# A decoder layer's mixing in five pieces of columns for six, with its feed-forward groups kept

## The chip, the cores and the metric

The kernel runs on one core of a Trainium2 chip. The metric is the device time of one execution in microseconds (us). A core has five engines, each with an instruction queue of its own that is worked off in order: the TensorE (PE, matmuls; PEld is its loading of weights), the VectorE (DVE), the ScalarE (ACT), the GpSimd (POOL) and the SyncE (SP), which here starts the DMA transfers. A median measured against the kernel before is told from no change from about 0.2% on.

## The reference

One layer of a hybrid decoder: RMSNorm, one input projection for four retention heads and four HGRN2 heads, their chunkwise recurrence, a gated output projection added to the input, RMSNorm, a squared-ReLU feed-forward of width 4096 added on, and a final RMSNorm. There are 2048 prompt tokens and 64 sample tokens (8 sequences of 8 with states of their own), 2112 in all; the model width is 1024. The outputs are the normed activations of both and the recurrences' final states.

```python
def mixer(h, pos, s_ret, s_hg, w_in, ret_norm_w, hgrn_norm_w, lb, w_out):
    proj = h @ w_in                                   # 1024 -> 4096 columns
    rq, rk, rv, rg, hq, hf, hi, hg = jnp.split(proj, idx, axis=-1)
    ...
    o_r, s_ret_new = chunk_gla(rq, rk, rv, log_g_ret, s_ret)
    ...
    o_h, s_hg_new = chunk_gla(hq, k_in, v_in, log_f, s_hg)
    ...
    o = jnp.concatenate([o_r, o_h], axis=-1).astype(h.dtype)
    return o @ w_out, s_ret_new, s_hg_new

def reference(...):
    ...
        hp = rmsnorm(xp, norm_mix_w[l])
        mp, sr_p, sh_p = mixer(hp, pos_p, zero_ret, zero_hg, ...)
        xp = xp + mp
        hp = rmsnorm(xp, norm_ffn_w[l])
        xp = xp + jnp.square(jax.nn.relu(hp @ w_up[l])) @ w_down[l]
    ...
    y_prompt = rmsnorm(xp, final_norm_w)
```

## The kernel before

**Precision.** All products are of 32-bit floats. Each operand is cut into a high part (a cast on the ScalarE) and a low part (the rest, a subtraction on the VectorE), and a product is three matmuls: high by high, high by low, low by high. Weights are cut as they arrive, 128 x 1024 at a time: hi at L271 on the ScalarE, lo at L285 on the VectorE, from a buffer `raw` that a transfer of 512 KB fills.

**Groups.** The tokens are columns. They are worked on in three groups of T = 640, 768 and 64 + 640 = 704 (the last with the sample tokens), first all groups through the mixing, then all through the feed-forward. [...] `proj()` (L342) makes one block of 128 output rows: for each of the operands, for each of the three part products, a matmul for each piece, into one of two banks `pj`.

**Mixing.** A group goes through `norm_in`, the heads' projections and recurrences, and `out_proj`. `norm_in` of the next group runs beside `out_proj` of this one: for each of eight blocks the ScalarE makes a high part (L546), the VectorE a low part (L547), the ScalarE a square and the VectorE its sum (L530). `residual()` makes the first seven heads' share of eight output blocks, 21 part products each, and adds the input (L1204); `out_proj` then adds the eighth head's share (L1249), stores the sum as `res` and scaled by the norm's weights as `in` in DRAM, one store for each of eight blocks. For the first group the squares are summed apart, on POOL and VectorE (L530, L600), and a matmul with ones makes their column sums (L570).

**Feed-forward.** It is a Strassen-like scheme of seven products for eight. Activations are quartered by rows and by halves of columns, B11 to B22; `plan_operands` sums them (L1291) and cuts the sums (L1280 on the ScalarE, L1284 on the VectorE) into the operands T3, T2, T1, T4 of the products, two row blocks each. `product()` (L1189) is 24 matmuls of T/2 columns. `up_two` starts a group with the fourteen products of the first two blocks of the width: B11, B11, B21, B22, B21, B22, then T2, T3, T1, T4 twice; a product's two banks are in `pj` or `pf`. T4's product adds onto T3's bank after T3 was read, by the second add at L1406 (u3, followed on the VectorE by the sum at L1436).

**The end of a group.** `finish()` makes the final norm of a feed-forward group, while the next group's feed-forward runs: eight squares (ACT, L1625), six adds and two adds of a guard term (DVE, L1627 and L1630), two splits (ACT L1356, DVE L1357), column sums by eight matmuls (L1365), two factors (ACT, L1676), sixteen products (DVE, L1643), and eight stores of y on SP.

**What sets the order.** Nothing is put in order by hand. Work beside the matmuls is put on an agenda by `later(ticks, ...)`, and a tick passes with every operand of `proj` (three part products) and with every two matmuls of the feed-forward. So for `finish()`, `begin`, `pace`, `wait` and `each` are ticks after the next group's start: a square every `pace` from `begin`, a product every `each` from `wait`, and a tick of the feed-forward is two matmuls. Engines run their queues in the order in which the program issues, so an instruction that waits holds up all behind it.

**Memory.** A tile of T columns takes one of 44 slabs of 768 columns; there are six load buffers of the same width. Weights in the feed-forward are loaded to a pool `raw` of 3 buffers or, two positions in seven of three each, a pool `sum` of 4 (by the weight's number, k % 7 % 2).

## Time and profile before

| | |
|---|---|
| median of 3 runs | 2508.93 us (2508.18 to 2508.98) |
| the profiled execution | 2508.95 us |
| its span, first to last instruction | 2507.2 us |
| granted TensorE clock | 0.999 |
| busy: PE, DVE, ACT, POOL | 2494.0, 1878.1, 1253.9, 366.1 us |
| DMA moved | 525.39 MB, mean 210 GB/s |

A row of the timeline gives the start of an instruction in us from the span's start, its duration in us, its engine and line, the operation, the tiles that it writes and reads with their sizes, how many alike follow each other, and in brackets how long the engine sat idle before it and who ended that. Tile names are the program's with their buffer's number left out: `slab` any of the slabs, `pj` and `pf` the banks of matmul results, `ld` a load buffer, `hi`, `lo` and `raw` a weight's parts and source. A row of the chain gives a start, a time and the number of instructions in it. Windows give a stretch's length and each engine's busy time in it, with the number of instructions in brackets. Line numbers are those of the kernel before; the changed file's are a little higher (L342 is L345, L285 is L288, L1204 is L1214, L1406 is L1421, L1643 is L1658).

### The profile page before, as it was taken

How to read it: one execution, taken by the hardware profiler on the slowest of the kernel's cores; microseconds unless marked ns; L12 is line 12 of the kernel's file. 1: busy time of each engine (PE TensorE's matmuls, PEld its weight loads, DVE VectorE, ACT ScalarE, POOL GpSimd, SP SyncE). 2: the span in 40 equal slices, each digit the busy share in tenths (PEclk: the TensorE clock that was granted, in tenths of full speed). 3: DMA queues.
4: the chain of work that ended last, by engine and by line, in shares of the span. 5: the costliest groups of instructions: out<-in, count | busy, mean ns of one | idle time of the engine just before them, and what ended most of it. 6: DMA issues, size and time to landing. Idle time of an engine off the chain costs nothing.

```text
span 2507.2 us, 41510 instructions
## 1 busy us (share of the span) xinstructions
PE 2494.0 (99%) x16593; PEld 2474.9 (99%) x16593; DVE 1878.1 (75%) x2443; ACT 1253.9 (50%) x1674; POOL 366.1 (15%) x304
## 2 busy tenths in 40 slices
PE   9999999999999999999999999999999999999998
PEld 9999999999999999999999999999999999999998
DVE  7666865668684766677775899775699878678987
ACT  6665653444463444443644555444454436445544
POOL 5223304324411432340000000000000000000000
PEclk9999999999999999999999999999999999999999
DMA  7454563465575565758866856566675546867552
GB/s 269 164 185 168 209 225 135 160 228 185 199 244 212 194 215 195 264 206 306 305 216 213 284 198 213 173 237 221 202 261 177 189 148 202 274 192 247 192 187 88
DMA packets 189073, 525.39 MB, mean 210 GB/s; under 512 B 18640, under 2 KB 59856, under 8 KB 188880
## 3 DMA queue, kind: packets, MB, share of 16 engines
q1 hardware_dynamic: 188736, 522.73, 60.6%
q8 instruction: 130, 2.13, 0.3%
q14 instruction: 63, 0.52, 0.1%
q10 hardware_dynamic: 144, 0.02, 0.0%
HBM read 389.50 MB, written 132.38 MB: 208 GB/s over the span
## 4 chain that ended last, share of the span: by engine, by line
PE 96%; DVE 3%; ACT 1%; issue 1%; DMA 0%; DVEq 0%; ACTq 0%
PE pj L342 27%; PE pf L1189 26%; PE pj L1189 25%; PE pjv L732 8%; PE mm L898 1%; PE po L1078 1%; PE mm L1086 1%; PE po L1080 1%; PE mm L955 1%; PE mm L509 1%; PE mm L510 1%; PE mm L1012 1%; PE mm L830 0%; PE po L764 0%; DVE raw L1221 0%
## 5 line engine op out<-in xcount | busy, mean ns | idle before, releaser
L271 ACT CAST hi<-raw 128x1024 fp32r<-128x1024 f32 x392 | 413.1, 1054 | 610.0 <-PE pf L1189 261.4
L342 PE MATMUL pj<-slab,hi 128*128 128x320 f32 (+2 forms) x3072 | 661.5, 328 | 2.6 <-DVE slab L644 1.3
L1189 PE MATMUL pf<-slab,hi 128*128 128x320 f32 (+2 forms) x2768 | 659.1, 321 | 0.0
L1189 PE MATMUL pj<-slab,hi 128*128 128x352 f32 (+2 forms) x2608 | 622.1, 322 | 0.0
L285 DVE TENSOR_TENSOR lo<-raw,hi 128x1024 fp32r<-128x1024 f32 x392 | 485.3, 1238 | 111.9 <-ACT hi L271 105.8
L342 PEld LDWEIGHTS pj<-slab,hi 128*128 128x128 f32 x3072 | 508.1, 188 | 5.3 <-DVE slab L644 1.5
L1189 PEld LDWEIGHTS pf<-slab,hi 128*128 128x128 f32 x2768 | 481.9, 188 | 0.0
L1189 PEld LDWEIGHTS pj<-slab,hi 128*128 128x128 f32 x2608 | 454.5, 188 | 0.1
L1189 PE MATMUL pf<-slab,lo 128*128 128x320 f32 (+2 forms) x1384 | 445.5, 322 | 0.0
L1189 PE MATMUL pj<-slab,lo 128*128 128x352 f32 (+2 forms) x1304 | 420.3, 322 | 0.0
L342 PE MATMUL pj<-slab,lo 128*128 128x320 f32 (+2 forms) x1536 | 379.1, 328 | 0.4 <-DVE lo L285 0.4
L342 PEld LDWEIGHTS pj<-slab,lo 128*128 128x128 f32 x1536 | 263.3, 188 | 1.3 <-DVE lo L285 0.9
L1189 PEld LDWEIGHTS pf<-slab,lo 128*128 128x128 f32 x1384 | 260.3, 188 | 0.0
L1189 PEld LDWEIGHTS pj<-slab,lo 128*128 128x128 f32 x1304 | 245.3, 188 | 0.0
L732 PE MATMUL pjv<-hi,slab 128*128 128x256 f32 x1088 | 204.8, 285 | 0.0
L1280 ACT CAST slab<-slab 128x640 fp32r<-128x640 f32 (+2 forms) x192 | 145.7, 780 | 65.8 <-DVE slab L1291 52.2
L1284 DVE TENSOR_TENSOR slab<-slab 128x640 fp32r<-128x640 f32 (+2 forms) x192 | 167.3, 886 | 8.9 <-PE pj L1189 3.2
L732 PEld LDWEIGHTS pjv<-hi,slab 128*128 128x128 f32 x1088 | 172.2, 192 | 1.5 <-issue 0.2
L732 PE MATMUL pjv<-lo,slab 128*128 128x256 f32 x544 | 153.8, 283 | 0.0
L879 ACT ACTIVATE slab<-slab 128x640 f32<-128x640 f32 (+2 forms) x72 | 56.4, 784 | 154.6 <-POOL slab L875 154.4
L732 PEld LDWEIGHTS pjv<-lo,slab 128*128 128x128 f32 x544 | 104.2, 192 | 0.0
L1536 DVE TENSOR_TENSOR slab<-pf,slab 128x640 f32<-128x640 f32 (+2 forms) x88 | 77.6, 888 | 29.6 <-PE pf L1189 29.1
(218 smaller groups left out, 3004.1 us busy)
## 6 DMA issues: line engine op xcount, KB each, us to landing
raw<-w SPq DMA_DIRECT2D x264, 512.0 KB, 4.2
slab<-u SPq DMA_DIRECT2D x32, 384.0 KB, 4.7
u<-ld SPq DMA_DIRECT2D x30, 384.0 KB, 3.7
slab<-u SPq DMA_DIRECT2D x32, 352.0 KB, 4.5
u<-ld SPq DMA_DIRECT2D x30, 352.0 KB, 4.0
slab<-u SPq DMA_DIRECT2D x32, 320.0 KB, 4.5
u<-ld SPq DMA_DIRECT2D x30, 320.0 KB, 3.9
ld<-x SPq DMA_DIRECT2D x16, 384.0 KB, 3.6
```

The source lines that it names most:

```text
L271: self.nc.scalar.copy(hi, raw)
L285: self.nc.vector.tensor_tensor(out=lo, in0=self.second.pop(j), in1=hi.bitcast(F32), op=ALU.subtract)
L342: self.nc.tensor.matmul(pj[:, i, :T2], w, a[:, c0:c1], start=j == 0 and q == 0, stop=j == n - 1 and q == 2)
L509: self.nc.tensor.matmul(ps, self.ones_r, hi, start=True, stop=False)
L510: self.nc.tensor.matmul(ps, self.ones_r, lo, start=False, stop=True)
L732: nc.tensor.matmul(pj[:, i * 256:(i + 1) * 256], a[:, s:s + C], ww, start=kb == 0 and q == 0, stop=kb == KB - 1 and q == 2)
L879: nc.scalar.activation(x["dd", w][:, a:T], x["dd", w][:, a:T], AF.Exp)
L898: nc.tensor.matmul(ps[:, j * P:(j + 1) * P], qk[:, cols[c]], qk[:, cols[c]], start=True, stop=True)
L1189: self.nc.tensor.matmul(*a, **k)
L1280: self.nc.scalar.copy(hi[:, :g.T], B[name][:, :g.T])
L1284: self.nc.vector.tensor_tensor(out=lo[:, :g.T], in0=B[name][:, :g.T], in1=hi.bitcast(F32)[:, :g.T], op=ALU.subtract)
L1536: nc.vector.tensor_tensor(out=r, in0=ps, in1=r, op=ALU.add)
```

## The change

The mixing's groups become T = 512, 768 and 64 + 768 = 832. The first is one piece of 512 columns, the others two of 384 and of 416. The feed-forward keeps 640, 768 and 704, now as `FF_GROUPS`. What the mixing hands on in DRAM (`res` and `in`) is therefore kept in tiles between the edges 0, 512, 640, 1280, 1408 and 2112 of either grouping: the second and the third group store each block in two parts (32 more stores in all), and a load of a quarter that crosses an edge comes in two parts. Slabs grow to 832 columns and are 41 for 44, load buffers grow alike, `raw` has 2 buffers for 3 and shares by k % 3. `finish()` of the first two feed-forward groups starts at ticks 10 and 60 for 96 and 200, with closer steps. y is stored with its columns in one order for all groups.

```diff
@@ -26,8 +26,8 @@
 FF = 4096
 EPS = 1e-6
 C = 128
-SLAB = 768
-NSLAB = 44
+SLAB = 832
+NSLAB = 41
 NLD = 6
 LEVELS = (64, 32, 16, 8, 4, 2)
 NLV = len(LEVELS) + 2
@@ -35,8 +35,11 @@
-GROUPS = ((0, 0, 640), (0, 640, 768), (NS, 1408, 640))
+GROUPS = ((0, 0, 512), (0, 512, 768), (NS, 1280, 768))
 NT = NS + SEQ
+FF_GROUPS = ((0, 640), (640, 768), (1408, 704))
+
+EDGES = (0, 512, 640, 1280, 1408, NT)
 WT = 1024
 N_IN, N_OUT, N_UP, N_DN = 32, 8, 32, 32
 W_OUT0 = N_IN
@@ -259,9 +262,9 @@
                 if self.stream[self.w_load][0] == "p":
                     break
                 k, later = self.w_load, self.w_load >= self.n_sums
-                other = later and k % 7 % 2
+                other = later and k % 3
                 raw = self.raws[k] = self.wp.tile([P, WT], F32, tag="sum" if other else "raw", name="raw",
-                                                  bufs=4 if other else 3)
+                                                  bufs=4 if other else 2)
                 e = self.stream[k]
                 self.fetch(raw, self.sums[e[1]] if e[0] == "s" else self.I["w"][e[1]])
                 self.w_load += 1
@@ -426,6 +429,13 @@
                 g.pieces = [(0, g.T)] if g.T <= 512 else [(0, g.T // 2), (g.T // 2, g.T)]
                 g.segs = [list(range(first)), list(range(first, nch))]
                 gs.append(g)
+            fs = []
+            for off, T in FF_GROUPS:
+                g = type("G", (), {})()
+                g.i, g.off, g.T = len(fs), off, T
+                fs.append(g)
+            self.between = {(name, a): self.dp.tile([P, KB, e - a], F32, name=f"{name}{a}")
+                            for a, e in zip(EDGES, EDGES[1:]) for name in ("res", "in")}
             nc.scalar.dma_start(vec, I["vec"])
             nc.scalar.preload_act_table_set("natural_log_exp_and_others")
             self.norm_in(gs[0], True)
@@ -460,12 +470,12 @@
                 mixing.close()
                 self.pf = ctx.enter_context(tc.tile_pool(name="pf", bufs=2, space=bass.MemoryType.PSUM))
-            self.out_proj(gs[2], 3, lambda: self.prepare(gs[0], 12), end_of_mixing)
-            self.ffn(gs[0], lambda: self.prepare(gs[1], 8))
-            self.finish(gs[0], begin=96, pace=10, wait=200, each=8)
-            self.ffn(gs[1], lambda: self.prepare(gs[2], 8), 190)
-            self.finish(gs[1], begin=96, pace=10, wait=200, each=8)
-            self.ffn(gs[2], None, 190)
+            self.out_proj(gs[2], 3, lambda: self.prepare(fs[0], 12), end_of_mixing)
+            self.ffn(fs[0], lambda: self.prepare(fs[1], 8))
+            self.finish(fs[0], begin=10, pace=4, wait=60, each=5)
+            self.ffn(fs[1], lambda: self.prepare(fs[2], 8), 190)
+            self.finish(fs[1], begin=10, pace=4, wait=60, each=5)
+            self.ffn(fs[2], None, 190)
             nc.sync.dma_start(self.O["ret_p"].rearrange("h d v -> d h v"), self.S[:, :H])
             nc.sync.dma_start(self.O["hg_p"].rearrange("h d v -> d h v"), self.S[:, H:])
@@ -1242,22 +1252,27 @@
         nc, T = self.nc, g.T
         part = self.residual(g, when, beside)
         between()
-        g.res, g.in_ = (self.dp.tile([P, KB, T], F32, name=f"{name}{g.i}") for name in ("res", "in"))
         for n in N_ORDER:
             pj = self.proj(g, self.take(2), g.oc[H - 1])
             r, b = part[n], self.get()
             nc.vector.tensor_tensor(out=self.v2(r, g), in0=pj, in1=self.v2(r, g), op=ALU.add)
             nc.scalar.activation(b[:, :T], r[:, :T], AF.Copy, scale=self.vec[:, V_FFN + n:V_FFN + n + 1])
-            for kept, t in ((g.res, r), (g.in_, b)):
-                nc.sync.dma_start(kept[:, n], t[:, :T])
+            for name, t in (("res", r), ("in", b)):
+                for a, e in zip(EDGES, EDGES[1:]):
+                    if g.off <= a < g.off + T:
+                        nc.sync.dma_start(self.between[name, a][:, n], t[:, a - g.off:e - g.off])
         self.flush()
-    def quarter(self, g, src, v, m, h, into):
+    def quarter(self, g, name, v, m, h, into):
         n, w = 4 * m + 2 * v, g.T // 2
-        self.nc.sync.dma_start(self.pair(g, into), src[:, n:n + 2, h * w:(h + 1) * w])
+        c = g.off + h * w
+        for a, e in zip(EDGES, EDGES[1:]):
+            t0, t1 = max(a, c), min(e, c + w)
+            if t0 < t1:
+                self.nc.sync.dma_start(self.pair(g, into)[:, :, t0 - c:t1 - c], self.between[name, a][:, n:n + 2, t0 - a:t1 - a])
     def prepare(self, g, pace):
@@ -1265,7 +1280,7 @@
         def load(v, name):
             g.B[v][name] = self.load()
-            self.quarter(g, g.in_, v, *PLACE[name], g.B[v][name])
+            self.quarter(g, "in", v, *PLACE[name], g.B[v][name])
         for j, (name, v) in enumerate((name, v) for name in ("B11", "B21", "B22") for v in range(2)):
             first, second = self.halve(g, g.B[v], name, g.ops[v])
@@ -1295,7 +1310,7 @@
         def load(v, name):
             g.B[v][name] = self.load()
-            self.quarter(g, g.in_, v, *PLACE[name], g.B[v][name])
+            self.quarter(g, "in", v, *PLACE[name], g.B[v][name])
         for j, (name, v) in enumerate([(name, v) for v in range(2) for name in ("T3", "T2", "T1")] + [("T4", 0), ("T4", 1)]):
             self.later(10 + 8 * j, self.block_sum, g, g.B[v], name)
@@ -1315,7 +1330,7 @@
         def load(v, m, h):
             g.R[v][m, h] = self.get()
-            self.quarter(g, g.res, v, m, h, g.R[v][m, h])
+            self.quarter(g, "res", v, m, h, g.R[v][m, h])
         def square(v, m, h):
             t = self.get()
@@ -1663,8 +1678,9 @@
     def outputs(self, g, h):
-        o = KB * g.off
-        return self.O["y"][:, o:o + KB * g.T].rearrange("p (n h t) -> p n h t", n=KB, h=2)[:, :, h]
+        T2 = g.T // 2
+        a = g.off + h * T2
+        return self.O["y"].rearrange("p (n t) -> p n t", n=KB)[:, :, a:a + T2]
     def last_guard(self, g, q):
@@ -1796,7 +1812,7 @@
     samples, prompts, off = [], [], 0
     for ns, p0, n in GROUPS:
         T = ns + n
-        rows = y[:, KB * off:KB * (off + T)].reshape(P, KB, T).transpose(2, 1, 0).reshape(T, D)
+        rows = y.reshape(P, KB, NT)[:, :, off:off + T].transpose(2, 1, 0).reshape(T, D)
         samples.append(rows[:ns])
         prompts.append(rows[ns:])
         off += T
```

Two places in the order of the VectorE and one of the TensorE show what moves. First the TensorE at the program's beginning: the last of the first projection blocks' matmuls and the column sums of the squares (`mm`). Before:

```order
L342 MATMUL pj<-slab,hi 128x320 x4
L342 MATMUL pj<-slab,lo 128x320 x2
L342 MATMUL pj<-slab,hi 128x320 x4
L342 MATMUL pj<-slab,lo 128x320 x2
L570 MATMUL mm<-slab,ones 128x320 x2
L342 MATMUL pj<-slab,hi 128x320 x4
```

and now:

```order
L345 MATMUL pj<-slab,hi 128x512 x2
L345 MATMUL pj<-slab,lo 128x512
L345 MATMUL pj<-slab,hi 128x512 x2
L345 MATMUL pj<-slab,lo 128x512
L580 MATMUL mm<-slab,ones 128x512
L345 MATMUL pj<-slab,hi 128x512 x2
```

Two rows are an operand by a weight block, as before, with three matmuls for six; the column sums stand behind 66 matmuls for 132.

Second the VectorE at the start of the second feed-forward, from a sum for T4 to the second add at L1406 (L1421 in the change) and what follows. Before:

```order
L1291 TENSOR_TENSOR slab<-ld,slab 128x768
L285 TENSOR_TENSOR lo<-raw,hi 128x1024
L1284 TENSOR_TENSOR slab<-slab 128x768
L1406 TENSOR_TENSOR slab<-pj,slab 128x768
L285 TENSOR_TENSOR lo<-raw,hi 128x1024
L1630 TENSOR_TENSOR slab<-slab 128x320
L1436 TENSOR_TENSOR slab<-slab 128x768
L1406 TENSOR_TENSOR slab<-pj,slab 128x768
L285 TENSOR_TENSOR lo<-raw,hi 128x1024
L1627 TENSOR_TENSOR slab<-slab 128x640 x2
L1406 TENSOR_TENSOR ld<-pf,slab 128x768
L1406 TENSOR_TENSOR slab<-pf,slab 128x768
```

and now:

```order
L1658 SCALAR_TENSOR_TENSOR slab<-slab,vec 128x320 x3
L1299 TENSOR_TENSOR slab<-slab 128x768
L1306 TENSOR_TENSOR slab<-ld,slab 128x768
L1658 SCALAR_TENSOR_TENSOR slab<-slab,vec 128x320 x2
L288 TENSOR_TENSOR lo<-raw,hi 128x1024
L1299 TENSOR_TENSOR slab<-slab 128x768
L1658 SCALAR_TENSOR_TENSOR slab<-slab,vec 128x320 x2
L1421 TENSOR_TENSOR slab<-pf,slab 128x768
L1658 SCALAR_TENSOR_TENSOR slab<-slab,vec 128x320 x2
L288 TENSOR_TENSOR lo<-raw,hi 128x1024
L1658 SCALAR_TENSOR_TENSOR slab<-slab,vec 128x320 x4
L1421 TENSOR_TENSOR slab<-pf,slab 128x768
```

The sixteen products of the first group's final norm (L1643, now L1658) stand ahead of T3's eviction, twelve of them ahead of T2's; before they came after all of these. Its six adds and two splits (L1642, L1372) are further up, among the sums and cuts:

```order
L288 TENSOR_TENSOR lo<-raw,hi 128x1024
L1642 TENSOR_TENSOR slab<-slab 128x640
L1299 TENSOR_TENSOR slab<-slab 128x768
L1642 TENSOR_TENSOR slab<-slab 128x640
L1306 TENSOR_TENSOR slab<-ld 128x768
L288 TENSOR_TENSOR lo<-raw,hi 128x1024
L1642 TENSOR_TENSOR slab<-slab 128x640
L1372 TENSOR_TENSOR slab<-slab 128x640
L1299 TENSOR_TENSOR slab<-slab 128x768
L1306 TENSOR_TENSOR slab<-slab,ld 128x768
L288 TENSOR_TENSOR lo<-raw,hi 128x1024
L1372 TENSOR_TENSOR slab<-slab 128x640
```

Third the VectorE in the residual products of the first group, from the fourth eviction (L1204, now L1214) to the fifth and on. L547 and L530 are `norm_in` of the next group, L285 weights' cuts, L1174 and L350 the last head's gating and cuts. Before:

```order
L1204 TENSOR_TENSOR slab<-pj,ld 128x640
L530 TENSOR_TENSOR slab<-slab 128x768
L285 TENSOR_TENSOR lo<-raw,hi 128x1024
L547 SCALAR_TENSOR_TENSOR slab<-ld,vec,slab 128x768
L530 TENSOR_TENSOR slab<-slab 128x768
L1174 TENSOR_TENSOR slab<-slab 128x384
L547 SCALAR_TENSOR_TENSOR slab<-ld,vec,slab 128x768
L1174 TENSOR_TENSOR slab<-slab 128x384
L530 TENSOR_TENSOR slab<-slab 128x768
L1204 TENSOR_TENSOR slab<-pj,ld 128x640
```

and now:

```order
L1214 TENSOR_TENSOR slab<-pj,ld 128x512
L1184 TENSOR_TENSOR slab<-slab 128x256
L557 SCALAR_TENSOR_TENSOR slab<-ld,vec,slab 128x768
L1184 TENSOR_TENSOR slab<-slab 128x256
L540 TENSOR_TENSOR slab<-slab 128x768
L557 SCALAR_TENSOR_TENSOR slab<-ld,vec,slab 128x768
L1214 TENSOR_TENSOR slab<-pj,ld 128x512
L540 TENSOR_TENSOR slab<-slab 128x768
L353 TENSOR_TENSOR slab<-slab 128x512
L288 TENSOR_TENSOR lo<-raw,hi 128x1024
L353 TENSOR_TENSOR slab<-slab 128x512
L557 SCALAR_TENSOR_TENSOR slab<-ld,vec,slab 128x768
```

`norm_in`'s instructions (L557, L540) keep their 768 columns and the weights' cuts (L288) their 1024; the group's own are 512 and 256 wide for 640 and 384.

## The prediction

> **What bounds the kernel now.** First the page, its busy shares and the chain that ended last:
>
> ```profile
> PE 2494.0 (99%) x16593; PEld 2474.9 (99%) x16593; DVE 1878.1 (75%) x2443; ACT 1253.9 (50%) x1674; POOL 366.1 (15%) x304
> PE 96%; DVE 3%; ACT 1%; issue 1%; DMA 0%; DVEq 0%; ACTq 0%
> PE pj L342 27%; PE pf L1189 26%; PE pj L1189 25%; PE pjv L732 8%; PE mm L898 1%; PE po L1078 1%; PE mm L1086 1%; PE po L1080 1%; PE mm L955 1%; PE mm L509 1%; PE mm L510 1%; PE mm L1012 1%; PE mm L830 0%; PE po L764 0%; DVE raw L1221 0%
> ```
>
> The TensorE is the bound, nearly without a gap. Its waits (total us, times, longest) are the next view:
>
> ```profile
> PE pj L342 <- DVE slab L644: 1.3, 1, 1.3
> PE pj L342 <- ACT hi L271: 0.7, 1, 0.7
> PE pj L342 <- DVE slab L1204: 0.5, 1, 0.5
> ```
>
> So a matmul that is left out is worth its whole interval, and nothing else can be won: there is hardly any waiting to remove. The VectorE at 75% looks harmless, but that is an average; the windows (length, then busy time of PE, PEld, DVE, ACT, POOL, the granted clock, DMA share, GB/s) over the five stretches that the change touches say more:
>
> ```profile
> 7.93:27.24 19.31, 19.30 (x128) 18.89 (x129) 16.54 (x15) 14.77 (x20) 6.06 (x3) 1.00 0.81 304
> 302.60:341.70 39.10, 39.10 (x283) 39.09 (x282) 35.70 (x63) 27.70 (x43) 1.50 (x1) 1.00 0.66 216
> 713.10:760.10 47.00, 46.48 (x294) 46.19 (x293) 40.08 (x60) 26.12 (x40) 0.00 (x0) 1.00 0.76 258
> 1593.04:1630.50 37.46, 37.46 (x218) 37.46 (x217) 28.94 (x31) 23.36 (x28) 0.00 (x0) 1.00 0.54 174
> 2062.70:2097.30 34.60, 34.60 (x217) 34.60 (x216) 24.78 (x28) 20.96 (x27) 0.00 (x0) 1.00 0.54 178
> ```
>
> They are the start, the residual products of groups 0 and 1, and the starts of the second and third feed-forward. In the second row the VectorE works 35.70 of 39.10 us.
>
> **The matmuls saved.** The projection's matmuls (L342) take, by the chain of waits, in runs of 320, 384, 352 columns, and the values' (L732) of 256:
>
> ```profile
> 75.14 5.87 PE pj L342 x40
> 437.39 6.96 PE pj L342 x40
> 893.81 4.75 PE pj L342 x30
> 111.55 14.03 PE pjv L732 x117
> ```
>
> That is 146.8, 174.0, 158.3 and 119.9 ns each: columns at 2.4 per ns (133.3, 160.0, 146.7, 106.7) and a rest of 13.2 to 14.0 that doesn't grow with the columns. I take 13.3, and so 226.7 ns for 512 columns and 186.7 for 416, an estimate by that line. Each group has 768 products of a weight block with an operand half at L342, in two pieces 1536 matmuls, 4608 in the three groups; group 0's 512 columns go in one piece, so 768 + 2 x 1536 = 3840 are left, over the same columns in all. Gain: 768 x 13.3 ns = **10.2 us**. Hardly anything in the rows speaks for less than 9 or more than 11.
>
> [...]
>
> **Start of the second feed-forward.** The change calls finish() with begin=10, wait=60 where it was 96 and 200, and so puts group 0's final norm (six adds L1627, two splits L1357, sixteen products L1643) in among the sums L1291 and lower halves L1284 that the VectorE makes for the products T2, T3, T1, T4. T4, the tenth product, adds onto T3's bank, so its first matmul waits for T3's eviction, the second add at L1406. Rows of the timeline (start, duration, idle before):
>
> ```profile
> 1598.34 1.23 DVE L285 TENSOR_TENSOR lo<-raw,hi 128x1024 fp32r<-128x1024 f32 x1 [2.93 <-ACT hi L271]
> 1599.77 0.96 DVE L1284 TENSOR_TENSOR slab<-slab 128x768 fp32r<-128x768 f32 x1 [0.21 <-ACT slab L1280]
> ...
> 1602.50 1.23 DVE L285 TENSOR_TENSOR lo<-raw,hi 128x1024 fp32r<-128x1024 f32 x1 [0.90 <-ACT hi L271]
> ...
> 1606.37 0.96 DVE L1284 TENSOR_TENSOR slab<-slab 128x768 fp32r<-128x768 f32 x1 [0.91 <-ACT slab L1280]
> ...
> 1614.98 1.23 DVE L285 TENSOR_TENSOR lo<-raw,hi 128x1024 fp32r<-128x1024 f32 x1 [0.79 <-ACT hi L271]
> ...
> 1618.85 0.96 DVE L1284 TENSOR_TENSOR slab<-slab 128x768 fp32r<-128x768 f32 x1 [0.91 <-ACT slab L1280]
> ...
> 1626.55 0.96 DVE L1406 TENSOR_TENSOR slab<-pj,slab 128x768 f32<-128x768 f32 x1 [0.59 <-PE pj L1189]
> ```
>
> ```profile
> 1650.71 0.82 DVE L1357 TENSOR_TENSOR slab<-slab 128x640 fp32r<-128x640 f32 x1
> 1651.44 0.95 DVE L1381 SCALAR_TENSOR_TENSOR slab<-slab 128x768 f32<-128x768 f32 x1
> 1652.31 0.95 DVE L1406 TENSOR_TENSOR ld<-pj,slab 128x768 f32<-128x768 f32 x1
> 1667.26 2.40 DVE L1643 SCALAR_TENSOR_TENSOR slab<-slab,vec 128x320 f32<-128x320 f32 x5
> 1669.57 0.95 DVE L1464 TENSOR_TENSOR slab<-pf,slab 128x768 f32<-128x768 f32 x1
> ```
>
> ```profile
> 1630.51 0.51 PE L1189 MATMUL pj<-slab,hi 128*128 128x384 f32 x2
> ```
>
> Back to back, instructions start closer than their durations: 0.73 us for a 640-wide one (1650.71 to 1651.44), 0.87 for 768 (1651.44 to 1652.31), 0.46 for L1643 (five in 2.31). The adds at L1627 are 640 wide like L1357. Now 6 x 0.73 + 2 x 0.73 + 16 x 0.46 = 13.2 us come ahead of T3's eviction, and the sum at L1436 (0.87) goes behind it: 12.3 more. The idle stretches quoted after the first, 4.3 us, can take part of it; the first (2.93) can't, as by the order all of this work stands behind the lower half that ends it. The eviction, done before at 1627.5, is done at 1627.5 + 12.3 - 4.3 = 1635.5. T4 began at 1630.51, and the eight matmuls of the norm's column sums now ahead of it take 8 x 0.147 = 1.2: 1631.7. Loss 3.8, taken as **4 us**; 2.5 if L1643's stores and the ScalarE's squares leave no new holes, 6 if half of the old holes stay, since the stores are queued on SP ahead of weight loads.
>
> **Start of the third.** The same with a 768-wide norm and 704-wide operands, and with less cover:
>
> ```profile
> 2070.50 1.22 DVE L285 TENSOR_TENSOR lo<-raw,hi 128x1024 fp32r<-128x1024 f32 x1 [0.85 <-ACT hi L271]
> ...
> 2093.70 1.22 DVE L285 TENSOR_TENSOR lo<-raw,hi 128x1024 fp32r<-128x1024 f32 x1 [1.04 <-ACT hi L271]
> ...
> 2096.91 0.88 DVE L1406 TENSOR_TENSOR slab<-pj,slab 128x704 f32<-128x704 f32 x1
> ```
>
> ```profile
> 2138.71 1.67 DVE L1643 SCALAR_TENSOR_TENSOR slab<-slab,vec 128x384 f32<-128x384 f32 x3
> 2140.33 0.89 DVE L1464 TENSOR_TENSOR ld<-pf,slab 128x704 f32<-128x704 f32 x1
> ```
>
> ```profile
> 2097.89 0.55 PE L1189 MATMUL pj<-slab,hi 128*128 128x352 f32 x2
> ```
>
> The eviction ended at 2096.91 + 0.88 = 2097.8 and T4 began 0.1 later: no slack is left today. There come in 6 x 0.87 + 2 x 0.87 + 16 x 0.54 (three in 1.62) = 15.6 us; between the two rows of L285 seven idle stretches of 0.85 to 1.04 lie, 7 us in all. Eviction at 2106.4, T4 ready at 2097.9 + 8 x 0.174 = 2099.3: 7.1, and with a few tenths of new holes **7.5 us**; bounds 5 and 9.
>
> **Residual products of group 0.** norm_in of group 1 runs on the VectorE beside them, 768 wide as before, but a product block now passes in 21 x 0.2267 = 4.8 us instead of 42 x 0.1468 = 6.2. In the window of 39.10 us lie six blocks, 37.0, and 2.1 of other matmuls; now 28.6 + 2 = 30.6. The VectorE's 35.70 there shrinks less: by the order, two small copies and two state updates fewer (0.7), nine evictions and halves of 640 to 512 columns (0.13 each by the step from 768 to 640: 1.2), six of 384 to 256 and two left behind the stretch (1.7): 32.1. It is now the longer one, with 3.4 us in which it sat idle in that window, mostly for the ScalarE. Two banks cover one block's lateness, and before they were needed already:
>
> ```profile
> 302.59 0.82 DVE L1204 TENSOR_TENSOR slab<-pj,ld 128x640 f32<-128x640 f32 x1
> 333.20 0.82 DVE L1204 TENSOR_TENSOR slab<-pj,ld 128x640 f32<-128x640 f32 x1
> ```
>
> Four blocks (24.7 us of matmuls and up to 2.1 others) apart, but 30.6 us: 4 of the 6.2 were used. With 4.8 of cover and 32.1 + 3.4 against 30.6 I take **5 us**; 0 if holes and cover swallow it, 8 if the VectorE carries lateness in from the mixing ahead.
>
> **Smaller terms.** Residual products of group 1: norm_in of group 2 grows from 704 to 832 columns, fifteen instructions by 0.13 = 2 us in a window where 40.08 of 47.00 are busy and where L342 waited for L1204 already (the row of 0.5): **2 us**, 0 to 3.
>
> The start: the column sums L570 wait for a chain of squares and adds:
>
> ```profile
> 26.01 0.82 DVE L600 TENSOR_TENSOR slab<-slab 128x640 f32<-128x640 f32 x1
> 27.24 1.24 PE L570 MATMUL mm<-slab,ones 128*128 128x320 f32 x4
> ```
>
> Slack 0.4. The 128 matmuls ahead (19.3 us) become 64 x 0.2267 = 14.5, 4.8 us earlier; the chain, from 6 to 26.8, shrinks by at most a fifth where it is 640 wide and not at all in the weights' 1024-wide cuts, by some 2 us. So 4.8 - 0.4 - 2 = **2.5 us**, 0 to 3.5.
>
> Mixing of group 2: operations 832 wide for 704 beside matmuls slower in step (186.7 for 158.3 ns), and 41 slabs for 44, so a buffer is taken again sooner after its last use; the 1.3 us at L644 may go: **1 us**, -1.5 to 4. The 32 more stores of out_proj, the loads in two parts and 2 raw buffers for 3 come to nothing: a weight's transfer takes 4.2 us, and the other buffers still let it be asked for two products ahead:
>
> ```profile
> raw<-w SPq DMA_DIRECT2D x264, 512.0 KB, 4.2
> ```
>
> If that cover goes, it is the last rival.
>
> **Sum.** Against the profiled execution's 2508.95 us (span 2507.2; the median of the runs, 2508.93, is the same): 2508.95 - 10.2 + 4 + 7.5 + 5 + 2 + 2.5 + 1 = 2520.75, so **2521 us**, 0.5% slower. All low ends give 2504.7, all high ends 2532.5.
>
> **Rivals.** *The holes swallow everything*: a quarter of the VectorE's time is idle, and if T3's evictions came before the norm's products, with the start and the residuals covered, the whole saving would stand: 2508.95 - 10.2 = 2499, faster. The point from which it decides: in before's times T3's evictions would have to end by 1631.7 and 2099.3. The quoted sums speak against it: at the third feed-forward 15.6 us must go into 7 us of holes. *Only the feed-forward pays*: the banks cover the residuals and the start; -10.2 + 4 + 7.5 gives 2510, no change by the bound of 0.2% (5 us) that a measurement can tell. The slack of one block speaks for it, the fifth eviction against. *The buffers*: with 2 raw buffers or 41 slabs a weight or a mixing operand comes late regularly; 0.1 us at each of the 264 loads is 26 us, with half of the other losses about 2540. The DMA share of 0.54 to 0.76 speaks against it. [...] That the pieces aren't really merged is excluded by the order, which has 3840 matmuls.
>
> **Numbers.** The forecast 0.62, only the feed-forward 0.16, all swallowed 0.12, buffers 0.07, fixed part 0.03. Faster 0.12, same 0.16, slower 0.72. The range: from 2506, which takes in most of the second case, to 2533, the sum of the high ends.
>
> **What would show it.** Right: L342's 512-column runs at 227 ns; waits of the TensorE on L1406's successor or on the cuts' sums at the two feed-forward starts, 3 to 6 and 5 to 9 us, with the VectorE full there; on L1204's successor in group 0's residuals; on L600's at some 23 us. Wrong: T4 starts without a wait, or waits on raw loads or slabs in group 2's mixing.

## The result, and the profile after

| | before | the change |
|---|---|---|
| median | 2508.8 us (4 runs, 2508.18 to 2508.98) | 2532.18 us (4 runs, 2530.57 to 2534.03) |
| ratio, 95% interval | | 1.0094 (1.0081 to 1.0107) |
| profiled execution; span | 2508.95; 2507.2 us | 2532.11; 2530.2 us |
| granted TensorE clock, mean | 0.999 | 0.997 |

Slower by 23.4 us, as forecast in its sign and inside the range, but at the range's upper end: 2521 was said. Of the runs below, one of `fac` (4105 us) and one of before's beside it (3489 us) were disturbed, and the ratios leave them out. First the changed kernel's page, the lines of busy time and the groups of projection matmuls (matmuls, busy time, mean of one, idle time ahead of them and who ended it):

```profile
PE 2497.2 (99%) x15823; PEld 2431.9 (96%) x15823; DVE 1877.1 (74%) x2444; ACT 1246.5 (49%) x1672; POOL 369.6 (15%) x304
...
L345 PE MATMUL pj<-slab,hi 128*128 128x384 f32 (+2 forms) x2560 | 655.1, 360 | 8.9 <-DVE slab L1214 5.2
```

The 770 fewer matmuls on PE are there (15823 for 16593), yet PE isn't busy for less but for 3.2 us more, and the span holds 33.0 us outside its busy time for 13.2. The shares of the other engines moved by a point, which tells nothing. The waits of the TensorE (total us, times, longest) say where:

```profile
PE pj L345 <- DVE slab L1214: 5.2, 5, 2.8
PE pj L1380 <- ACT slab L1371: 2.3, 2, 1.3
PE po L771 <- DVE AT L997: 2.2, 2, 1.2
PE pj L345 <- DVE slab L353: 2.1, 1, 2.1
PE mm L519 <- DVE AT L909: 1.5, 2, 1.2
PE pj L345 <- DVE slab L1258: 1.5, 2, 1.2
PE pf L1199 <- DVE slab L1421: 1.5, 2, 1.1
PE pf L1199 <- ACT hi L274: 1.4, 2, 0.8
```

The three rows quoted of before summed to 2.5 us. Now nearly each row names the VectorE or what the ScalarE does beside it. By stages, in windows of before (length, then busy time of PE, PEld, DVE, ACT, POOL, the granted clock, DMA): the start, group 0's end with its residual products, group 1's, all of group 2's mixing, and the starts of the second and the third feed-forward:

```profile
0.00:111.40 111.40, 109.18 (x788) 106.86 (x789) 80.12 (x123) 74.35 (x106) 41.17 (x38) 1.00 0.63 229
258.50:395.70 137.20, 137.00 (x958) 135.37 (x957) 90.59 (x135) 77.38 (x111) 30.82 (x23) 1.00 0.58 202
660.30:815.00 154.70, 154.18 (x1014) 152.61 (x1014) 102.86 (x144) 75.93 (x106) 37.10 (x25) 1.00 0.63 221
815.00:1197.60 382.60, 380.85 (x2745) 374.12 (x2745) 271.97 (x450) 172.15 (x283) 120.21 (x113) 1.00 0.67 232
...
1592.00:1640.00 48.00, 48.00 (x280) 48.00 (x279) 37.80 (x41) 28.84 (x35) 0.00 (x0) 1.00 0.55 177
...
2060.00:2126.00 66.00, 66.00 (x412) 65.91 (x411) 54.33 (x60) 41.22 (x51) 0.00 (x0) 1.00 0.55 184
```

and of the change:

```profile
0.00:93.30 93.30, 88.84 (x492) 74.08 (x493) 68.11 (x118) 67.20 (x103) 34.91 (x38) 1.00 0.74 252
210.50:332.80 122.30, 118.06 (x665) 102.84 (x664) 81.03 (x130) 71.02 (x110) 27.81 (x23) 1.00 0.66 221
597.10:759.40 162.30, 159.51 (x1015) 157.49 (x1014) 104.89 (x145) 77.92 (x106) 37.85 (x25) 1.00 0.62 214
759.40:1208.50 449.10, 443.50 (x2954) 434.08 (x2954) 305.88 (x470) 188.63 (x288) 138.28 (x113) 1.00 0.61 204
...
1592.00:1640.00 48.00, 46.60 (x280) 45.74 (x279) 39.48 (x49) 31.10 (x41) 0.00 (x0) 1.00 0.50 166
1640.00:2060.00 420.00, 418.98 (x2416) 418.35 (x2415) 324.70 (x337) 187.82 (x209) 0.00 (x0) 1.00 0.63 207
2060.00:2126.00 66.00, 61.21 (x345) 59.40 (x344) 54.50 (x66) 36.23 (x46) 0.00 (x0) 0.95 0.53 178
```

Length less PE busy is its idle time. It grows from 2.2 to 4.5 us at the start, 0.2 to 4.2 at group 0's end, 0.5 to 2.8 at group 1's, 1.8 to 5.6 in group 2, 0 to 2.4 from the second feed-forward's start on, 0 to 4.8 at the third's. These are low ends: in these profiles a matmul's duration is about twice its interval (0.32 us for one of 352 columns, 0.16 to the next start), so the first 0.2 us or so of each wait count as busy. Counted from start to start, gaps of more than 0.12 us beyond the matmul's own median interval sum to 35 us in the change and 6 before, the half clock below among them. 29 us more of gaps, less the 7 to 9 us of matmul time that `halves` shows below to be saved, are 20 to 22 of the 23.4 us; the rest is in smaller gaps.

The last row has something else: a clock of 0.95. Windows inside it, and one in group 2's mixing, and the matmuls of the first (start, duration):

```profile
2093.00:2100.70 7.70, 5.43 (x30) 4.50 (x30) 7.70 (x10) 7.42 (x11) 0.00 (x0) 1.00 0.79 290
2100.70:2104.10 3.40, 3.40 (x13) 3.40 (x12) 2.49 (x4) 1.36 (x4) 0.00 (x0) 0.51 0.55 157
...
1117.90:1124.40 6.50, 3.64 (x20) 2.59 (x18) 6.44 (x9) 5.30 (x8) 2.72 (x1) 1.00 0.99 353
1124.40:1127.90 3.50, 3.50 (x10) 3.36 (x11) 2.75 (x3) 0.72 (x1) 0.00 (x0) 0.52 0.70 218
```

```profile
2098.03 0.62 PE L1380 MATMUL pf<-slab,ones_r 128*128 128x384 f32 x2 [0.71 <-DVE slab L1372]
2099.70 0.62 PE L1380 MATMUL pj<-slab,ones_r 128*128 128x384 f32 x2 [1.05 <-ACT slab L1371]
...
2103.52 0.49 PE L1199 MATMUL pj<-slab,lo 128*128 128x352 f32 x1
2103.82 0.66 PE L1199 MATMUL pj<-slab,hi 128*128 128x352 f32 x2
```

After a stretch in which the TensorE idled for 2 to 3 of some 7 us, it ran at half clock for 3.4 us: a 352-column matmul started 0.30 us after the one before, for 0.16. Summing the excess over each matmul's own interval, such a spell costs 1.2 to 1.6 us; this execution has three, some 4.5 us in all, the one before has none between its start and its last matmul.

### The profile page after: what moved, and what is told of

It reads as the page before. It is cut to its first block, busy times and chain, and to the rows that moved or that the text cites. A ratio compares the mean times of both kernels' runs of the same rounds, so it can differ in the third digit from the quotient of the medians.

```text
span 2530.2 us, 40232 instructions
## 1 busy us (share of the span) xinstructions
PE 2497.2 (99%) x15823; PEld 2431.9 (96%) x15823; DVE 1877.1 (74%) x2444; ACT 1246.5 (49%) x1672; POOL 369.6 (15%) x304
## 5 line engine op out<-in xcount | busy, mean ns | idle before, releaser
L345 PE MATMUL pj<-slab,hi 128*128 128x384 f32 (+2 forms) x2560 | 655.1, 360 | 8.9 <-DVE slab L1214 5.2
L288 DVE TENSOR_TENSOR lo<-raw,hi 128x1024 fp32r<-128x1024 f32 x392 | 482.4, 1231 | 110.2 <-ACT hi L274 103.0
L345 PEld LDWEIGHTS pj<-slab,hi 128*128 128x128 f32 x2560 | 459.2, 188 | 30.6 <-issue 3.8
L1199 PEld LDWEIGHTS pj<-slab,hi 128*128 128x128 f32 x2608 | 455.0, 188 | 1.4 <-ACT hi L274 0.9
L345 PE MATMUL pj<-slab,lo 128*128 128x384 f32 (+2 forms) x1280 | 378.3, 360 | 0.9 <-DVE lo L288 0.9
L1199 PEld LDWEIGHTS pj<-slab,lo 128*128 128x128 f32 x1304 | 245.8, 188 | 0.0
L345 PEld LDWEIGHTS pj<-slab,lo 128*128 128x128 f32 x1280 | 233.5, 189 | 10.4 <-DVE lo L288 1.8
L889 ACT ACTIVATE slab<-slab 128x768 f32<-128x768 f32 (+2 forms) x72 | 55.9, 781 | 138.7 <-POOL slab L885 138.1
```

The costliest lines, as they stand in the source:

```text
L288: self.nc.vector.tensor_tensor(out=lo, in0=self.second.pop(j), in1=hi.bitcast(F32), op=ALU.subtract)
L345: self.nc.tensor.matmul(pj[:, i, :T2], w, a[:, c0:c1], start=j == 0 and q == 0, stop=j == n - 1 and q == 2)
L889: nc.scalar.activation(x["dd", w][:, a:T], x["dd", w][:, a:T], AF.Exp)
L1199: self.nc.tensor.matmul(*a, **k)
```

## The experiments

Medians, with the ratio to the kernel before of the same call, and the lengths of four stages in the profiled execution: group 0's, group 1's and group 2's mixing (to the first L732 of group 1, of group 2, and the first matmul of the feed-forward) and the feed-forward to the span's end. The last column says in which of the four the half-clock spells stand: g1 and g2 for the mixing of groups 1 and 2, ff for the feed-forward.

| kernel | median us | ratio (95%) | group 0 | group 1 | group 2 | feed-forward | half-clock spells |
|---|---|---|---|---|---|---|---|
| before | 2508.8 | | 395.7 | 419.3 | 382.6 | 1309.6 | none |
| the change | 2532.18 | 1.0094 (1.0081 to 1.0107) | 332.8 | 426.6 | 449.1 | 1321.7 | g2, ff, ff |
| early | 2520.59 | 1.0047 (1.0032 to 1.0062) | 395.6 | 419.2 | 382.6 | 1322.6 | ff, ff |
| late43 | 2527.56 | 1.0073 (1.0058 to 1.0088) | 333.9 | 428.4 | 456.6 | 1309.0 | g1, g2, g2, g2 |
| nosq | 2523.61 | 1.0057 (1.0040 to 1.0074) | 330.4 | 423.3 | 448.0 | 1320.1 | ff |
| halves | 2534.43 | 1.0106 (1.0091 to 1.0121) | 337.6 | 428.0 | 449.0 | 1318.7 | g1, g2 |
| n42 | 2538.54 | 1.0121 (1.0106 to 1.0136) | 333.3 | 426.4 | 447.3 | 1329.3 | ff, ff (6.8 and 10.2 us long) |
| pool | 2532.80 | 1.0096 (1.0081 to 1.0111) | 335.0 | 427.0 | 449.0 | 1320.4 | g1, g2 |
| shift | 2530.33 | 1.0087 (1.0072 to 1.0102) | 333.9 | 428.0 | 446.3 | 1320.1 | g1, ff |
| sqe | 2529.58 | 1.0085 (1.0068 to 1.0102) | 333.2 | 428.0 | 449.0 | 1318.6 | g1, g2 |
| fac | 2522.97 | 1.0057 (1.0036 to 1.0079) | 334.3 | 426.4 | 447.3 | 1313.1 | none |
| pace16 | 2525.48 | 1.0066 (1.0050 to 1.0082) | 330.2 | 423.8 | 449.0 | 1318.5 | g2 |
| bufs41 | 2526.60 | 1.0074 (1.0058 to 1.0090) | 394.9 | 419.2 | 388.4 | 1321.8 | g2, ff, ff |
| comb | 2511.83 | 1.0014 (1.0005 to 1.0023) | 330.4 | 423.7 | 445.7 | 1310.3 | none |

A stage of one execution can hold or lack a half-clock spell of 1.2 to 1.6 us, and group 0's length differs by 1.1 us between the change and `shift`, whose code is the same there. So differences below 2 us in one stage are read only with this in view. The expectations count the feed-forward to its last matmul, some 8.4 us less than the table: 1301.2 us before, 1313.4 in the change.

**early: the timing of finish() alone, in the kernel before.**

```diff
-            self.finish(gs[0], begin=96, pace=10, wait=200, each=8)
+            self.finish(gs[0], begin=10, pace=4, wait=60, each=5)
```

(the same for gs[1])

> The kernel before, with finish() of the first two feed-forward groups moved to begin=10, pace=4, wait=60, each=5, as the change has it, and nothing else: 44 slabs of 768, six pieces, 3 raw buffers. Theory (the final norm's VectorE work ahead of T3's eviction makes T4 wait, and idle spells of the TensorE there halve its clock for some 3 us): 11 to 14 us over before, so 2520 to 2523 us, with waits on L1406, L1365 and the cuts at the second and third feed-forward starts and none elsewhere. Rival (the feed-forward's 12 us come from the 41 slabs, the two raw buffers or the split loads): within 3 us of before, 2508 to 2512.

2520.59 us, 11.9 over before; the mixing is before's to 0.2 us and the feed-forward 13 us longer. Its waits:

```profile
PE pj L1365 <- ACT slab L1356: 2.3, 2, 1.2
PE pf L1189 <- ACT hi L271: 1.5, 2, 0.9
...
PE pf L1189 <- DVE slab L1406: 1.2, 2, 0.8
...
PE pf L1365 <- DVE slab L1357: 0.7, 1, 0.7
```

The change's feed-forward loss is this one edit: this kernel has neither fewer slabs and buffers nor split loads, and it loses 13 us there for the change's 12.1, two half-clock spells among them in either. But the largest wait is not that of T4 on T3's eviction (1.2 us). It is the norm's column sums (L1365), which stand between the early products and wait for their splits.

**late43: the change with finish() at its old ticks.** By the count of tiles in use these ticks take 43 slabs, as the norm's operands would still hold slabs that the products' operands need; 43 fit when the load buffers are five. No run tried these ticks with 41.

```diff
-NSLAB = 41
-NLD = 6
+NSLAB = 43
+NLD = 5
...
-            self.finish(fs[0], begin=10, pace=4, wait=60, each=5)
+            self.finish(fs[0], begin=96, pace=10, wait=200, each=8)
```

> The change with finish() at its old ticks (begin=96, pace=10, wait=200, each=8), which takes 43 slabs for 41 and 5 load buffers for 6. Theory: the feed-forward's 12 us come back and the mixing keeps its loss, 2518 to 2522 us, the feed-forward 1300 to 1303 us long as before. Rival (slabs or raw buffers): the feed-forward stays above 1308 us, the time above 2527. If the fifth load buffer is needed, a loss shows as waits on ld in the mixing, up to 5 us.

2527.56 us: the feed-forward is back at before's length, 1309.0, which settles that part from the other side. (To the last matmul it is 1300.6 us, as the expectation has it.) The time is not where it was forecast, since group 2's mixing lost 7.5 us more. Two more half-clock spells there are some 3 us of it. A wait on a transfer into a load buffer is new, and so are two others, on the VectorE and the ScalarE; that the missing sixth buffer is behind these two as well is not shown:

```profile
PE mm L520 <- DVE slab L353: 2.8, 1, 2.8
...
PE po L774 <- DMA ld<-hg_s: 2.2, 2, 2.0
PE mm L797 <- ACT slab L794: 2.0, 1, 2.0
```

So the early finish() is what the wider slabs led to, and the memory that undoes it here was taken from another place that pays.

**nosq: norm_in without its seven adds.**

```diff
-                g.sq = self.add_square(g, g.sq, x, nc.vector)
+                if kb == 0:
+                    g.sq = self.add_square(g, None, x)
+                else:
+                    self.add_square(g, None, x)
```

> The change without the seven adds of squares (L540) in norm_in of groups 1 and 2; the squares themselves stay, so the norms of these groups are made from one block's square alone. Theory (the VectorE is the bound in the residual products): 6 to 7 us of VectorE work less in each of the two stretches takes the waits on L1214 and L1258 away, about 5 us at group 0 and 2.5 at group 1: 2523 to 2526 us. Rival (the two banks of results, the ScalarE or the shorter blocks themselves are the bound there): no change, 2531 to 2533.

2523.61 us, 8.6 less than the change: group 0 2.4 us shorter, group 1 3.3, and one spell in place of three. In the windows of the two residual stages

```profile
211.70:330.40 118.70, 116.77 (x666) 103.12 (x665) 75.48 (x123) 71.04 (x110) 26.82 (x23) 1.00 0.68 228
594.60:753.70 159.10, 159.10 (x1015) 157.50 (x1014) 99.05 (x138) 77.81 (x106) 37.63 (x25) 1.00 0.64 218
```

the TensorE's idle time falls from 4.2 to 1.9 and from 2.8 to 0 us, with 5.5 and 5.8 us of VectorE work gone; no wait on L1204's successor is left. The other 2.9 us lie outside these stages, where the profile has two spells fewer in all. The VectorE is the bound in the residual products.

**pace16: the same work, spread.**

```diff
-            self.out_proj(gs[0], 1, lambda: self.norm_in(gs[1], pace=12))
+            self.out_proj(gs[0], 1, lambda: self.norm_in(gs[1], pace=16))
```

(the same for gs[2])

> The change with norm_in of groups 1 and 2 spread over sixteen ticks a block for twelve, so that its VectorE work lies under all eight residual blocks and the last products. Theory (the rate of the VectorE's work beside the residual blocks is the loss there, 5 us at group 0 and 2.3 at group 1): 2 to 5 us of it come back, 2527 to 2530. Rival: the norm of the next group is late for its projection, the loss moves to the first projection blocks of groups 1 and 2, 2531 to 2536.

2525.48 us, 6.7 less than the change, with nothing left out. Group 0 is 2.6 us shorter and group 1 2.8, nearly as without the adds (the profiled execution also lacks both spells of the feed-forward, 3.2 us there). It is the rate of the work beside the blocks, not its amount, that the TensorE waited for; the next group's projection was not late for it.

**pool: the adds on GpSimd.**

```diff
-                g.sq = self.add_square(g, g.sq, x, nc.vector)
+                g.sq = self.add_square(g, g.sq, x)
```

> The change with norm_in's adds of squares (L540) of groups 1 and 2 on GpSimd for the VectorE. Theory (the VectorE's queue alone decides in the residual products): the same gain as without the adds, 2522 to 2527 us. Rival (the two engines slow each other: at the start of the kernel before, while POOL's three adds ran from 17.9 to 24.1 us, a cut L285 took 2.59 us for 1.23 and an add L530 2.1 for 0.81): the VectorE loses more than the adds it is spared, and the waits on L1214 stay or grow, 2530 to 2540 us.

2532.80 us, no gain; group 0 is 2.2 us longer. One of the adds moved to GpSimd, and the VectorE beside it:

```profile
275.47 1.95 POOL L540 TENSOR_TENSOR slab<-slab 128x768 f32<-128x768 f32 x1 [0.96 <-ACT slab L537]
```

```profile
276.25 2.26 DVE L288 TENSOR_TENSOR lo<-raw,hi 128x1024 fp32r<-128x1024 f32 x1
```

A cut of two inputs takes 2.26 us beside the add, against the 1.23 us that the same cut takes on the mean in the change. With seven adds gone from it, the VectorE is busy for longer in group 0's last stage, 83.35 us for the change's 81.03:

```profile
210.90:334.90 124.00, 117.91 (x665) 102.92 (x664) 83.35 (x123) 71.24 (x110) 41.29 (x30) 1.00 0.65 218
```

The cut ends 1.1 us after the add, at 278.51 us for 277.42, about its own time alone, as if it had worked only then. At the start of the kernel before it is the same: GpSimd's three adds end at 24.09 us and the cut L285 beside the last of them, 2.59 us long, at 25.17. What holds the cut up is not in these rows. Giving these adds to GpSimd spared the VectorE no time.

**halves: group 0 in two pieces of 256.**

```diff
-                g.pieces = [(0, g.T)] if g.T <= 512 else [(0, g.T // 2), (g.T // 2, g.T)]
+                g.pieces = [(0, g.T // 2), (g.T // 2, g.T)]
```

> The change with group 0's 512 columns in two pieces of 256, so with 4608 matmuls at L345 again. Theory by the fixed part of 13.3 ns: 768 x 13.3 = 10.2 us more on the TensorE, and less waiting at the start and in group 0's residual products (a block lasts 0.3 us longer), up to 2 us: 2540 to 2543 us. By the 229.7 ns that a 512-column matmul took in the change, against two of 119.9: 7.8 us, 2538 to 2541. [...]

2534.43 us, only 2.3 over the change and below both forecasts. The stages show why: group 0 takes 4.8 us more, with its gaps some 2 us smaller, so 7 us of matmul time; the feed-forward, the same code in the same order, takes 3.0 us less, as it has no half-clock spell here and two in the change. Runs of matmuls of L345 alone, of the change (512 columns, then 416) and of this kernel (256):

```profile
14.00:22.90 8.90, 8.90 (x40) 7.13 (x38) 1.00 0.78 277
723.34:759.40 36.06, 36.06 (x193) 35.65 (x192) 1.00 0.50 177
```

```profile
14.14:23.61 9.47, 9.47 (x80) 9.42 (x79) 1.00 0.78 265
```

One of each count belongs to the next start: 228.2, 187.8 and 119.9 ns. Two of 256 less one of 512 are 11.6 ns here and 9.1 by the means over all of them (119.4 and 229.7, gaps left out). The merging is worth 768 times that, 7 to 9 us, not the 2.3 between the medians, and somewhat less than 10.2.

**bufs41: 41 slabs and two raw buffers alone.** The kernel `early` with

```diff
-NSLAB = 44
+NSLAB = 41
...
-                other = later and k % 7 % 2
+                other = later and k % 3
...
-                                                  bufs=4 if other else 3)
+                                                  bufs=4 if other else 2)
```

> The kernel before with 41 slabs for 44, two raw buffers for three with the change's rule, and finish() early, as the change has them, but the groups of 640, 768, 704 and six pieces. Theory (slabs and raw buffers cost nothing by themselves; finish() does): as the kernel before with finish() early alone, 2519 to 2523 us, the mixing as before's to 1 us. Rival (buffers and slabs cost in the mixing): 3 us or more over that, with waits in the mixing of group 2.

2526.60 us, 6.0 over `early`; the theory fell. The mixing of group 2 takes 388.4 us for 382.6 (about 1 of it a half-clock spell), at 704 columns, the rest of the program as in `early`. The wait on L644 doubled, and one on L886 is new:

```profile
PE pj L342 <- DVE slab L644: 2.6, 1, 2.6
...
PE mm L898 <- DVE slab L886: 1.6, 1, 1.6
```

Both name the VectorE, though only slabs and buffers are fewer. I read it so that an instruction waits for a free one and holds up its engine's queue, and that the last link is the one shown; no row here shows the first link. Slabs and raw buffers were not taken apart.

**shift: group 2's weight sums 20 ticks later.**

```diff
-            self.plan_sums(sums[NQ:], at)
+            self.plan_sums(sums[NQ:], [a + 20 for a in at])
```

> The change with the weight sums (L1231) of group 2's mixing 20 ticks later. Theory (group 2's waits of the TensorE on L997, L353 and L896 come from sums that stand ahead of these on the VectorE, not from the slabs): the waits in the mixing of group 2 move, most of its 5 us beyond before's go or turn up elsewhere, 2526 to 2535 us. Rival (the slabs, or the width of 832 alone): the same waits at the same instructions, 2531 to 2533.

2530.33 us, 1.9 less. Group 2 is 2.8 us shorter: the waits on L997 at its first two heads are gone, a new one on L654 (1.1 us) stands at the third. But the change has a half-clock spell in this stage and `shift` none, some 1.5 of the 2.8 us; and `nosq`, also without one there and with the old order, takes 448.0 us for 446.3. So the order of the VectorE's queue is worth 1 to 2 us here, near the limit of what a stage can tell; by bufs41 memory is the larger part.

**sqe: the first squares ten ticks earlier.**

```diff
-                self.at(24 + 2 * kb, square, kb)
+                self.at(14 + 2 * kb, square, kb)
```

> The change with the squares of the first group begun ten ticks earlier. Theory (the column sums L580 and what follows wait for the chain of squares, started by ticks that are now shorter): 2 to 3.5 us of the start's loss come back, the first values' matmuls (L742) begin at 29 us or earlier for 31.1, 2528.5 to 2530.5. Rival (the ScalarE or the transfers of x bound the chain, whatever the tick): within 1 us of the change, 2531 to 2533.

2529.58 us, but not for that reason: the first values' matmuls begin at 33.7 us for 31.1, those of the second head at 93.7 us for 93.3, and the feed-forward is 3.1 us shorter without a spell. The start gained nothing.

**n42 and fac: the late products behind T3's eviction.** 42 slabs, which fit, allow products from tick 95 on (begin=24 in the first, 10 in the second). The second also issues the column sums earlier:

```diff
-            self.later(wait - 8 + 2 * h, factor, h)
+            self.later((wait - 8 if last else t1 + 12) + 2 * h, factor, h)
```

> The change with 42 slabs and finish() at begin=24, pace=4, wait=95, each=8: seven of the sixteen products L1658 go behind T3's eviction, the adds and splits stay ahead of it. Theory: 7 x 0.46 = 3.2 us less of the second feed-forward's loss and 7 x 0.54 = 3.8 less of the third's, one idle spell at half clock less or so: the feed-forward 1305 to 1308 us for 1313, the time 2524 to 2528 us. Rival (the adds and splits ahead of it are what costs, the wait at L1380 above all): the feed-forward 1310 or more, 2529 to 2533.

2538.54 us, worse: the column sums, issued eight ticks ahead of the products, now stood amid the next group's products T2 to T4 and waited for a bank that L1438 reads. The two half-clock spells behind these waits last 6.8 and 10.2 us, for 3.4 each in the change.

```profile
PE pf L1380 <- ACT slab L1438: 9.1, 2, 5.3
```

> The change with 42 slabs, finish() at begin=10, pace=4, wait=95, each=8, and its column sums (L1380) issued twelve ticks after the last square, not eight ticks ahead of the first product, so that they don't stand on the TensorE's queue in the middle of the late products, where the run n42 waited 9.1 us for a bank. Theory (the VectorE's list ahead of T3's eviction is the loss): without the sixteen products ahead of it the feed-forward loses 3 to 7 us for 12.3, 1304 to 1308 us long, the time 2523 to 2528. Rival (any column sums in this place wait for a bank or for the splits): the feed-forward above 1310, the time above 2529.

2522.97 us, 9.2 less than the change, the feed-forward 8.6 us shorter, some 3 of it the two spells that are gone. No wait on L1421 is left; those of the column sums are, 3.5 us:

```profile
PE pj L1380 <- ACT slab L1371: 2.3, 2, 1.3
...
PE pf L1380 <- DVE slab L1372: 0.7, 1, 0.7
PE pf L1380 <- ACT slab L1371: 0.5, 1, 0.5
```

**comb: all that helped.** `fac` with the column sums at t1 + 18, `pace16`, `shift` and `sqe`.

> All mends that helped, together, on the change: 42 slabs with the late products and column sums eighteen ticks after the last square, norm_in over sixteen ticks a block, the weight sums of group 2 twenty ticks later, the squares of the first group ten ticks earlier. Theory (the losses stand at separate places and add up): from the 2532.2 us of the change come off 9.2 (late products and column sums), 6.7 (norm_in), 1.9 (weight sums) and 2.6 (squares), so 2511.8, and up to 3.5 more if the column sums no longer wait for their splits: 2508 to 2513, level with the kernel before or just over it. Rival (each mend moves its wait to the next place): 2516 or more.

2511.83 us over 11 runs, 1.0014 of before (1.0005 to 1.0023): the loss is cut from 23.4 to 3.3 us, and the kernel before is not beaten. The feed-forward is at 1310.3 us for before's 1309.6, and no half-clock spell is left in its profile. What stays is mostly in the mixing and outweighs the 7 to 9 us saved: idle time of 5.0 us for before's 2.2 to the second head, 2.3 for 0.2 at group 0's end, 3.6 for 1.8 in group 2. That the sum of the single gains was met to the digit is luck, as `sqe`'s part was a spell.

## Why the prediction was right, and where not

- **The bound and the sign**: right. Fewer matmuls, and waits on the VectorE at the places where its work became dense.
- **The matmuls saved, 10.2 us**: 7 to 9. The constant rest of 13.3 ns gave 226.7 and 186.7 ns; 228.2 to 229.7 and 187.8 to 188.0 were measured. The rest wasn't constant in the rows quoted either: 158.3 ns at 352 columns leave 11.6, not 13.2 to 14.0. That row was off: over all of before's matmuls the interval there is 161 ns, so a rest of 14.3. At 2.4 columns per ns the rest grows a little with the columns, to 15 or 16 ns at 512; against the 0.03, the fixed part is there at the larger widths too. The rows quoted give 2.37 columns per ns from 256 to 384 (128 more in 54.1 ns); by that line 512 columns take 228.1 ns, as measured, and the merging saves 9.0 us.
- **Second feed-forward, 4 us; third, 7.5**: 2.4 us of idle time in the windows from 1592 to 2060 us, and 4.8 plus some 3 of half clock. `early` gives 13 us for both together, forecast were 11.5, without half clock. The sum over the VectorE's list was the right tool; its place was half wrong. Behind T3's eviction, on which the sum was made, the TensorE waited 0.4 and 1.1 us. I counted the eight column sums of the second as 1.2 us of work; over both starts they took 3.5 us of waits, ahead of the list's end. All waits at the two starts sum to 2.6 and 4.9 us; 3 to 6 and 5 to 9 were named as the sign. (Ten of the norm's sixteen products, not twelve, stood ahead of T2's eviction; all sixteen stood ahead of T3's, so the sum is the same.)
- **Residual products of group 0, 5 us, and of group 1, 2 us**: 4.0 and 2.3 more idle time. `nosq` and `pace16` show the cause. That 5 came so near is in part luck: 32.1 + 3.4 against 30.6 is 4.9 before any cover, and what was left of a block's 4.8 us of cover was not taken off.
- **The start, 2.5 us**: 2.2 us more idle time, but not at the column sums L580, which hardly waited. The largest wait was that of a matmul (L519) behind a masked copy,

```profile
PE mm L519 <- DVE AT L909: 1.2, 1, 1.2
```

  and the cause of the rest was not isolated.
- **Group 2's mixing, 1 us**: the step that failed most. 3.8 us more idle time and some 1.5 of half clock. The bounds held -1.5 to 4. The 41 slabs were named in this term, but no price was worked out for them, and the raw buffers were put at nothing because a weight's transfer, 4.2 us in the row quoted, was put at less than two products' time. `bufs41` shows that 41 slabs and two raw buffers cost about 5 us in this very stage without any wider tile; which of the two it is stays open. So the rival of the buffers, given 0.07 as a loss at every load, came true in part, as a few long waits.
- **Half clock after waits, not in the sum**: some 4.5 us. The waits I forecast were priced at their length alone. With it and with group 2 right, 2521 would have been about 2528, and with 2 us less saved about 2530.
- **The range**: that it held 2532 is in part luck. Its upper end was all high ends together; most of the terms came out near their middle, and what filled the gap was half clock and group 2.

## What to carry to other kernels

Where the bounding engine has no gaps, making it faster anywhere shortens the time in which the others' work must pass: add up the other engines' queues for each such stretch, between the results that the bounding engine waits for, not for the kernel as a whole. Wider tiles are paid for in their number, and what then has to move earlier can cost more than the tiles gain (13 us by `early`, for 7 to 9 gained). Work that is spread over a longer stretch can give back as much as work that is left out (5.4 us in groups 0 and 1 by `pace16`, 5.7 by `nosq`).

## What the runs showed of the hardware

Idle time of the TensorE costs more than its length, but not always. At the same instruction, a residual block of group 1 that waits 2.8 us for an eviction, the change went on at full clock and `sqe` at half:

```profile
692.50:696.00 3.50, 3.50 (x20) 3.50 (x21) 3.50 (x4) 0.98 (x2) 0.00 (x0) 1.00 0.95 360
```

```profile
693.10:696.50 3.40, 3.40 (x13) 3.40 (x12) 3.40 (x5) 0.98 (x2) 0.00 (x0) 0.50 0.86 340
```

So 13 matmuls in 3.4 us for 20 in 3.5. Every spell in the table lasts 3.4 us, but for n42's of 6.8 and 10.2, twice and three times that. In `sqe` the clock fell after this single wait of 2.8 us; in the change, at the third feed-forward's start, after three of 0.5 to 1.1 us with matmuls between. Neither brings it about each time: the change kept full clock after the first, and `fac`, whose waits of 0.5 to 1.3 us at the same column sums sum to 3.5 us over both starts, has no spell. What decides is not shown here. Half clock is also a cause at hand for the wider spread of the kernels that wait: 3.5 us over four runs of the change, 0.8 over those of before; that was not tried by itself.
